# A hybrid attention block: the relative-position line is written to DRAM once, and the banded branch takes its query rows in falling order

## The chip, the core and the metric

The kernel runs on one core of a Trainium2 chip. The core has five engines that work side by side, each through its own queue in order: PE (TensorE, matrix products; PEld is its weight load), DVE (VectorE), ACT (ScalarE), POOL (GpSimd) and SP (SyncE, which here only issues DMAs; ACT's queue issues some as well). 16 DMA engines move the data. The metric is the device time of one run in microseconds (us); lower is better.

## What is computed

One block of a network on 512 tokens of width 1024, in float32. A normalised input is projected to four branches; each branch output is projected to 1024 columns, multiplied by a sigmoid gate of its own, and the four are added, projected once more and added to the input. A gated feed-forward layer of width 2816 follows. The branches are a softmax attention with a forget term ("fox", 4 heads), a short convolution, a chunked linear attention ("mlstm") and an attention in a sliding window of 128 tokens ("swa", 8 query heads, 2 key heads). The change is about the last one, whose scores have a bias that depends on the distance of query and key alone:

```
dist = arange(128)[:, None] + 128 - arange(256)[None, :]       # query row, key column of the band
swa_bias = rel_bias[t5_bucket(maximum(dist, 0))]                # per head, 128 x 256
s = q @ k_band.T * d**-0.5 + swa_bias                           # 4 blocks of 128 queries, 256 keys each
s = where(0 <= dist < 128 and key exists, s, -inf)
p = softmax(concat(s, sink))[..., :-1]
out = p @ v_band
```

A query in row i and a key in column j of the band have the distance i + 128 - j, so one line of 384 values per head, indexed by j - i + 127, holds every bias and the mask.

## The kernel before, in words

Every product of float32 data is made of three matmuls over split operands: a value is split into a rounded high part (`hi`, an ACT copy, L133) and the rest (`lo`, a DVE subtract, L134), and `mm3` (L127 to L130) multiplies hi by hi, hi by lo and lo by hi. Weights come as a stream of 512 KB tiles that SP loads into 3 buffers (`w_load`, L157); each tile has two halves that `w_split` splits on ACT and DVE, up to 6 halves ahead of use. A buffer takes the next load when both of its halves are split.

`proj` (L395) makes one block of 128 output columns for all 512 tokens: 8 steps of three matmuls of 512 columns. The order of the program is: the first projections (value and gate logits), fox keys and queries with their head norms (`head_normed`), the three conv projections `pcu`, `pcc`, `pcb` for two halves, the conv branch's gates (`gated("conv")`, tiles `gconv` for the gate and `oconv` for the branch output) with the fox attention running in the background, the swa keys and queries, the fox gates with the swa attention in the background, the mlstm projections, the swa gates, the mlstm gates, merge and feed-forward. The order on each engine's queue isn't that of the text: a planner simulates the program and sets the order of each queue; at run time each queue is worked off strictly in that order.

The bias line: `swa_bias_line` (L364) makes the 8 x 384 line with one matmul (`pl`), copies it to SBUF (`ln`), and one DMA on ACT's queue writes it 128 times into a DRAM tensor `d_line` of 128 x 8 x 384 (L371). The DMA's outer dimension is the 8 heads, each of which is one SBUF partition. `swa_bias_load` (L374), right ahead of the swa projections, loads four tiles `bw` of 128 x (2 heads x 256): partition i starts one element earlier in its own copy than partition i - 1 in its, so a row of 256 slides along the line (L377).

The swa queries: `q_stack` (L406) puts hi over lo for each head into a tile `sq..q` of 128 partitions by 512 tokens, with one ACT copy and one DVE subtract. In `swa_attention`, `scores` (L536) multiplies 128 queries (as the stationary operand) with the keys of the band, a DVE instruction adds the bias tile and takes the row maximum (L555), and exp, row sum and scaling follow; `transposes` (L574) turns the probabilities so that keys lie on the partitions; `values` (L583) multiplies them with the values, adds the two halves of the result on DVE (`sw`, L596) and splits the sum into the branch output `ysh`, `ysl` (L599), 128 tokens at a time.

Of the kernel before, what the change touches and what calls it, by code (L numbers as in the profile page):

```python
# [8 lines left out]
F32 = mybir.dt.float32  # L9
# [3 lines left out]
ALU = mybir.AluOpType  # L13
# [3 lines left out]
P = 128  # L17
# [10 lines left out]
LW = 384  # L28

FOX_H, ML_H, SWA_H, SWA_KV = 4, 4, 8, 2  # L30
# [14 lines left out]
def kernel(  # L45
# [11 lines left out]
    nc = tc.nc  # L57
# [4 lines left out]
    dram = ctx.enter_context(tc.tile_pool(name="dram", bufs=1, space=DRAM))  # L62
# [4 lines left out]
    def s_tile(name, dt=F32):  # L67
        return big.tile([P, NT], dt, tag="s", name=name, bufs=N_S)

    def wk(name, dt=F32):  # L70
        return big.tile([P, NT], dt, tag="wk", name=name, bufs=N_WK)
# [4 lines left out]
    def ps_at(name):  # L76
        return psum.tile([P, NT], F32, tag="at", name=name, bufs=8 - TUNE["mm"])
# [16 lines left out]
            else:  # L94
                nc.sync.dma_start(wr[-1], w_tok[ko // 2])

# [1 line left out]
    ident = const.tile([P, P], F32, name="ident")  # L98
    make_identity(nc, ident)
    ident_bf = const.tile([P, P], BF16, name="ident_bf")  # L100
# [18 lines left out]
    qgain = const.tile([P, 2], F32, name="qgain")  # L119
    nc.gpsimd.tensor_scalar(qgain[:, 0:1], col[:, C_FQ:C_FQ + 1], HD ** -0.5, None, op0=ALU.mult)  # L120
    nc.gpsimd.tensor_scalar(qgain[:, 1:2], col[:, C_SQ:C_SQ + 1], HD ** -0.5, None, op0=ALU.mult)

# [1 line left out]
    def nc_table(name):  # L124
        tc.keep_in_program_order(nc.scalar.preload_act_table_set(name))

# [5 lines left out]
    def split(hi, lo, src):  # L132
        nc.scalar.copy(hi, src)  # L133
        nc.vector.tensor_tensor(lo, src, hi.bitcast(F32), op=ALU.subtract)  # L134

    def scaled_split(hi, lo, src, scale):
        nc.scalar.activation(hi, src, AF.Copy, scale=scale)
        nc.vector.scalar_tensor_tensor(
            lo, src, scale, hi.bitcast(F32), op0=ALU.mult, op1=ALU.subtract)
# [5 lines left out]
        nc.vector.scalar_tensor_tensor(t, t, -0.5, v, op0=ALU.mult, op1=ALU.mult)  # L145
        nc.vector.scalar_tensor_tensor(out, t, 1.5, y0, op0=ALU.add, op1=ALU.mult)

# [1 line left out]
    n_w = w_str.shape[0]  # L149
    stream = {"raw": 0, "split": 0, "raws": [], "ready": []}  # L150

# [26 lines left out]
    def w_blk(w, j, n=P):  # L178
        return w[0][:, j * n:(j + 1) * n], w[1][:, j * n:(j + 1) * n]

    # work that rides along with the projections: `later` runs a piece after a number of
    # product steps, `background` advances one stage of an attention every `period` of them
    background, deferred = [], []
    pace = {"period": 4, "count": 0}

    def later(steps, fn):
        deferred.append([steps, fn])
# [24 lines left out]
        while len(background) > keep:  # L212
            bg()

    # ---- the array runs at its full clock once it has been busy for a while: keep it so
    # while the first loads are on their way ----
    warm = const.tile([P, NT], BF16, name="warm")
    nc.vector.memset(warm, 0.0)
    pw = ps_mm("warm_ps")
    for _ in range(TUNE["warm"]):  # L220
        nc.tensor.matmul(pw, warm[:, 0:P], warm, start=True, stop=True)

# [1 line left out]
    xg = []  # L224
    ssq = wk("ssq")
    ps_n = [ps_at(f"psn{t}") for t in range(NB)]
    for ko in range(KO):
# [7 lines left out]
        for t in range(NB):  # L235
            tb = slice(t * P, (t + 1) * P)
# [3 lines left out]
        else:  # L240
            sq = wk(f"xsq{ko}")
# [36 lines left out]
    nsnk = const.tile([P, SWA_H], F32, name="nsnk")  # L278
    nc.gpsimd.tensor_scalar(nsnk, snk, -1.0, None, op0=ALU.mult)

    # token-major results: fox v, swa v, gate logits
    vf = [s_tile(f"vf{t}", F32R) for t in range(NB)]
    vs2 = [s_tile(f"vs{i}", F32R) for i in range(2)]
    vs = [vs2[t // 2][:, (t % 2) * 256:(t % 2) * 256 + 256] for t in range(NB)]
# [3 lines left out]
    for t in range(NB):  # L288
        r1 = rcol[:, t:t + 1]
        for v, c0, n in ((vf[t], 0, FOX_H), (vs[t], 256, SWA_KV)):  # L290
            vv = v.rearrange("p (h u d) -> p h u d", h=n, u=2)
            src = ps_n[t][:, c0:c0 + n * HD].rearrange("p (h d) -> p h d", h=n)
# [2 lines left out]
        nc.vector.tensor_scalar(  # L295
            gdst, ps_n[t][:, 384:396].rearrange("p (a b) -> p a b", b=4), r1, None, op0=ALU.mult)

# [1 line left out]
    d_rows = dram.tile([12, NT], F32, name="d_rows")  # L299
    acol = const.tile([P, NB, 4], F32, name="acol")  # L300
    negc, negm, gexp = [], [], []
# [55 lines left out]
                    bass.AP(d_rows.tensor, d_rows.offset + (8 + 2 * p + j) * NT, [[0, HD], [1, NT]]))  # L357
            gexp.append(t)

# [1 line left out]
    d_line = dram.tile([P, SWA_H, LW], F32, name="d_line")  # L361
    biasw = []

    def swa_bias_line():  # L364
        pl = ps_at("pl")
        nc.tensor.matmul(pl[0:SWA_H, 0:LW], rb, oh, start=True, stop=True)
        ln = wk("ln")
        nc.vector.tensor_copy(ln[0:SWA_H, 0:LW], pl[0:SWA_H, 0:LW])
        src = ln[0:SWA_H, 0:LW]
        src = bass.AP(src.tensor, src.offset, [src.ap[0], [0, P], [1, LW]])  # L370
        nc.scalar.dma_start(d_line.rearrange("p h w -> h p w"), src)  # L371
        yield

    def swa_bias_load():  # L374
        for i in range(4):
            t = s_tile(f"bw{i}")
            nc.scalar.dma_start(  # L377
                t.rearrange("p (h k) -> p h k", h=2),
                bass.AP(d_line.tensor, d_line.offset + 127 + 2 * i * LW,
                        [[SWA_H * LW - 1, P], [LW, 2], [1, 256]]))  # L380
            biasw.append(t)

# [1 line left out]
    xn = []  # L384

    def normed_input(ko):
# [4 lines left out]
        scaled_split(h, l, t, col[:, C_AN + ko:C_AN + ko + 1])  # L391
        xn.append((h, l))

# [1 line left out]
    def proj(name, moving=None):  # L395
        ps = ps_mm(name)
        mv = moving or xn
        for ko in range(KO):
            if ko % 4 == 0:
                w = w_take()  # L400
            mm3(ps, w_blk(w, ko % 4), mv[ko], ko == 0, ko == KO - 1)
            tick()
        return ps

# [1 line left out]
    def q_stack(name, src, scale=1.0):  # L406
        out = []
        for j in range(2):
            own, oth = slice(j * HD, j * HD + HD), slice(HD - j * HD, P - j * HD)
            t = s_tile(f"{name}q{j}", F32R)  # L410
            if scale == 1.0:
                split(t[own], t[oth], src[own])
            else:
                scaled_split(t[own], t[oth], src[own], scale)
            out.append(t)
        return out
# [13 lines left out]
    def head_normed(name, ps, gain, eps, then):  # L430
        qg, sq = s_tile(f"{name}g"), s_tile(f"{name}s")
        nc.scalar.activation(sq, ps, AF.Square)
        nc.scalar.activation(qg, ps, AF.Copy, scale=gain)
        s2 = sum_split(name, sq)
        later(TUNE["norm_lag"], lambda: head_normed_rest(name, qg, sq, s2, eps, then))
# [20 lines left out]
        nc.gpsimd.tensor_tensor(qg, qg, sq, op=ALU.mult)  # L456
        then(qg)

# [1 line left out]
    y = {}  # L460

    def pt_split(name, src, n):
# [62 lines left out]
    def swa_attention():  # L525
        ysw = []
        for g in range(SWA_KV):
            t = [big.tile([P, 2, NT], F32R, tag="ysw", name=f"ys{n}{g}", bufs=4) for n in "hl"]
# [54 lines left out]
        def values(b, g):  # L583
            k0, nk = keys(b)
            po = ps_at(f"so{b}_{g}")
            for kk in range(nk):
                vv = vs[k0 // P + kk][:, g * P:(g + 1) * P]
                th = trans.pop((b, g, kk))
                nc.tensor.matmul(po, vv, th[0], start=kk == 0, stop=False)
                nc.tensor.matmul(po, vv, th[1], start=False, stop=kk == nk - 1)  # L590
            tmp, ys = wk(f"sv{b}_{g}"), wk(f"sw{b}_{g}")
            nc.scalar.copy(tmp[0:HD], po[HD:P])
            pov, tmv = (t.rearrange("p (i j t) -> p i j t", i=2, j=2) for t in (po, tmp))
            ysv = ys[:, 0:256].rearrange("p (i t) -> p i t", i=2)
            for j in range(2):
                nc.vector.tensor_tensor(ysv[j * HD:(j + 1) * HD], pov[0:HD, :, j, :], tmv[0:HD, :, j, :], op=ALU.add)  # L596
            yh, yl = ysw[g]
            tb = slice(b * P, (b + 1) * P)
            split(yh[:, :, tb], yl[:, :, tb], ysv)  # L599

        items = [(b, g) for b in range(NB) for g in range(SWA_KV)]
        yield from staged(items, (0, scores), (TUNE["swa_t"], transposes), (TUNE["swa_v"], values))
# [58 lines left out]
        items = [(2 * pair + j, b) for j in range(2) for b in range(NB)]  # L661
        yield from staged(items, (0, scores), (TUNE["ml_v"], values), (TUNE["ml_n"], normed))

# [1 line left out]
    y["fox"], y["conv"], y["swa"], y["mlstm"] = [], [], [], []  # L665
    fq, fk, sq_, sk, mq, mk, mo, vm = [], [], [], [], [], [], [], []
    gr, bl = gate_rows(), swa_bias_line()
# [5 lines left out]
    for p in range(2):  # L673
        ps = proj(f"pfk{p}", xg)
        head_normed(f"fk{p}", ps, col[:, C_FK:C_FK + 1], epsv, lambda k, p=p: fk.append(k_stack(f"fk{p}", k)))
        ps = proj(f"pfq{p}", xg)
        head_normed(f"fq{p}", ps, qgain[:, 0:1], epsv, lambda q, p=p: fq.append(q_stack(f"fq{p}", q)))

# [1 line left out]
    for p in range(2):  # L680
        ps = proj(f"pcu{p}")
        u = wk(f"cu{p}")
        nc.scalar.copy(u, ps)
        ps = proj(f"pcc{p}")
# [9 lines left out]
        ps = proj(f"pcb{p}")  # L694
        nc.vector.tensor_tensor(u, ps, u, op=ALU.mult)
        yh, yl = s_tile(f"ych{p}", F32R), s_tile(f"ycl{p}", F32R)
# [35 lines left out]
    gated("conv", False)  # L732
    flush()

# [1 line left out]
    swa_bias_load()  # L736
    nc_table("natural_log_exp_and_others")
    ps = proj("psk")
    head_normed("sk", ps, col[:, C_SK:C_SK + 1], None, lambda k: sk.extend(k_stack("sk", k)))
    for p in range(4):  # L740
        ps = proj(f"psq{p}")
        head_normed(f"sq{p}", ps, qgain[:, 1:2], None, lambda q, p=p: sq_.append(q_stack(f"sq{p}", q)))

    gated("fox", False, TUNE["swa_p"], swa_attention)

# [1 line left out]
    wv = [w_take() for _ in range(4)]  # L747
    for t in range(NB):
        ps = ps_mm(f"pmv{t}")
        tb = slice(t * P, (t + 1) * P)  # L750
        for ko in range(KO):
            w = wv[ko // 2]
# [7 lines left out]
        src = ps[:, 0:256].rearrange("p (g u d) -> p g u d", g=2, u=2)  # L760
# [4 lines left out]
    for p in range(2):  # L765
        ps = proj(f"pmk{p}")
        mk.append(k_stack(f"mk{p}", ps))
        ps = proj(f"pmq{p}")
        mq.append(q_stack(f"mq{p}", ps, HD ** -0.5))
        ps = proj(f"pmo{p}")  # L770
        t = s_tile(f"mo{p}")
# [8 lines left out]
    flush()  # L780
    gated("mlstm", True)

# [1 line left out]
    x2, x2g = [], []  # L784
    ssq2 = wk("ssq2")
    for d in range(KO):
        xr = wk(f"xr{d}")
        nc.scalar.dma_start(xr, xT[d * P:(d + 1) * P, :])
        ps = proj(f"mg{d}", merged)
        t = s_tile(f"x2_{d}")  # L790
# [7 lines left out]
        else:  # L798
            sq = wk(f"x2sq{d}")
            nc.scalar.activation(sq, t, AF.Square)  # L800
            nc.gpsimd.tensor_tensor(ssq2, ssq2, sq, op=ALU.add)

# [1 line left out]
    r2 = s_tile("r2")  # L804
    act = []
    for f in range(FB):
# [13 lines left out]
    w, j = None, 0  # L820
    for d in range(KO):
        ps = ps_mm(f"dn{d}")
        for f in range(FB):
            if j % 4 == 0:
                w = w_take()
# [3 lines left out]
        n = NT // 2 if d == KO - 1 else NT  # L829
# [11 lines left out]
def _layout(inputs):  # L841
    import numpy as np

    i = {k: np.asarray(v) for k, v in inputs.items()}
# [65 lines left out]
    cols[32:36, C_GB] = i["mlstm_f_bias"][0]  # L910
    cols[64:68, C_GB] = i["mlstm_i_bias"][0]

    # bucket of each distance: depends on shapes alone
    oh = np.zeros((33, LW), np.float32)
    n = np.arange(P)
    large = 16 + (np.log(np.maximum(n, 1).astype(np.float32) / np.float32(16))
                  / np.float32(np.log(8.0)) * np.float32(16)).astype(np.int32)
    bucket = np.where(n < 16, n, np.minimum(large, 31))
# [33 lines left out]
```

## Time and profile before

| what | value |
|---|---|
| time, median of 3 runs | 872.1 us (871.13 to 874.33) |
| span of the profiled execution, first to last instruction | 871.3 us |
| PE busy | 850.4 us (98%) |
| DVE busy | 493.5 us (57%) |
| ACT busy | 385.7 us (44%) |
| POOL busy | 145.1 us (17%) |
| mean granted TensorE clock | 0.990 |
| HBM read, written | 84.53 MB, 3.69 MB |

The profile gives the profiled execution by its span. A busy PE is one with a matmul in it, at whichever clock was granted (1.0 is 2.4 GHz, 0.5 is 1.2 GHz). Idle time of an engine costs something only where the work that sets the end waits for it; the table averages over stages with different limits.

### The profile page before, as it was taken

What the parts mean: (1) busy time and instruction counts of PE and PEld (TensorE: products, weight loads), DVE (VectorE), ACT (ScalarE), POOL (GpSimd) and SP (SyncE); (2) the same over time, 40 slices, a digit from 0 to 9 for tenths busy, and PEclk for the clock granted to TensorE, in tenths of its full rate; (3) what the DMA queues carried; (4) which work ended last, traced back from release to release, by engine and by line L of the source; (5) the groups of instructions that cost most, each with busy time, mean ns of one, the idle gap of its engine ahead of it and who ended that gap; (6) DMA issues with size and microseconds to landing.
All of it is one profiled execution on the core that took longest, in us unless ns stands there. A gap on an engine that the chain in (4) does not pass through costs nothing.

```text
span 871.3 us, 10668 instructions
## 1 busy us (share of the span) xinstructions
PE 850.4 (98%) x3879; PEld 701.1 (80%) x3879; DVE 493.5 (57%) x899; ACT 385.7 (44%) x733; POOL 145.1 (17%) x134
## 2 busy tenths in 40 slices
PE   7999799999999999999999999999999999999998
PEld 5867578888788888888888888888888888888886
DVE  6899576548888886577644545444444433432320
ACT  7565455457665765454544444333333322322210
POOL 5253000013311101222221212111111111000000
PEclk9999899999999999999999999999999999999999
DMA  6644422242222422222224432222222322233310
GB/s 229 212 145 86 109 97 73 73 145 73 73 73 72 147 73 96 73 74 97 96 97 128 151 108 97 98 97 97 97 97 97 97 96 97 97 121 108 121 37 24
DMA packets 29537, 88.91 MB, mean 102 GB/s; under 512 B 3456, under 2 KB 6049, under 8 KB 29485
## 3 DMA queue, kind: packets, MB, share of 16 engines
q1 hardware_dynamic: 24716, 80.87, 27.5%
q10 hardware_dynamic: 4768, 7.37, 3.8%
q8 instruction: 30, 0.49, 0.2%
q14 instruction: 23, 0.18, 0.1%
HBM read 84.53 MB, written 3.69 MB: 101 GB/s over the span
## 4 chain that ended last, share of the span: by engine, by line
PE 83%; DVE 7%; DMA 3%; ACT 2%; issue 2%; SPq 0%; POOL 0%; DVEq 0%; ACTq 0%; POOLq 0%
PE dn L130 5%; PE fu L130 5%; PE fg L130 5%; PE dn L129 5%; PE fu L128 5%; PE fg L128 5%; PE fu L129 5%; PE fg L129 5%; PE dn L128 5%; DMA wr<-in_w_str_dram 2%; PE gswa L129 2%; PE gswa L128 2%; PE gswa L130 2%; PE gmlstm L128 2%; PE gmlstm L130 2%
## 5 line engine op out<-in xcount | busy, mean ns | idle before, releaser
L134 DVE TENSOR_TENSOR wl<-wr,wh 128x512 fp32r<-128x512 f32 x278 | 202.9, 733 | 163.9 <-ACT wh L133 162.6
L133 ACT CAST wh<-wr 128x512 fp32r<-128x512 f32 x278 | 170.3, 619 | 273.5 <-PE dn L129 69.1
L129 PE MATMUL fu<-x2l,wh 128*128 128x512 f32 x176 | 68.5, 389 | 0.0
L128 PE MATMUL fu<-x2h,wh 128*128 128x512 f32 x176 | 68.5, 389 | 0.0
L130 PE MATMUL fg<-x2h,wl 128*128 128x512 f32 x176 | 68.5, 389 | 0.0
L130 PE MATMUL fu<-x2h,wl 128*128 128x512 f32 x176 | 68.5, 389 | 0.0
L128 PE MATMUL fg<-x2h,wh 128*128 128x512 f32 x176 | 68.5, 389 | 0.0
L129 PE MATMUL fg<-x2l,wh 128*128 128x512 f32 x176 | 68.5, 389 | 0.0
L128 PE MATMUL dn<-ah,wh 128*128 128x512 f32 x176 | 68.5, 389 | 0.0
L129 PE MATMUL dn<-al,wh 128*128 128x512 f32 x176 | 68.5, 389 | 0.0
L130 PE MATMUL dn<-ah,wl 128*128 128x512 f32 x176 | 68.5, 389 | 0.0
L815 POOL TENSOR_TENSOR ut<-ut,gt 128x512 f32<-128x512 f32 x22 | 34.3, 1560 | 204.6 <-DVE ut L814 175.7
L130 PEld LDWEIGHTS fg<-x2h,wl 128*128 128x128 f32 x176 | 33.1, 188 | 6.9
L129 PEld LDWEIGHTS fu<-x2l,wh 128*128 128x128 f32 x176 | 33.1, 188 | 6.9
L128 PEld LDWEIGHTS dn<-ah,wh 128*128 128x128 f32 x176 | 33.0, 188 | 6.9
L129 PEld LDWEIGHTS dn<-al,wh 128*128 128x128 f32 x176 | 33.0, 188 | 6.9
L129 PEld LDWEIGHTS fg<-x2l,wh 128*128 128x128 f32 x176 | 33.0, 188 | 6.9
L128 PEld LDWEIGHTS fu<-x2h,wh 128*128 128x128 f32 x176 | 33.1, 188 | 6.8
L130 PEld LDWEIGHTS fu<-x2h,wl 128*128 128x128 f32 x176 | 33.0, 187 | 6.9
L130 PEld LDWEIGHTS dn<-ah,wl 128*128 128x128 f32 x176 | 33.0, 188 | 6.7
L128 PEld LDWEIGHTS fg<-x2h,wh 128*128 128x128 f32 x176 | 33.0, 188 | 6.7
L814 DVE TENSOR_TENSOR ut<-fu,r 128x512 f32<-128x512 f32 x22 | 15.2, 691 | 29.9 <-PE fu L130 29.9
(598 smaller groups left out, 1936.0 us busy)
## 6 DMA issues: line engine op xcount, KB each, us to landing
wr<-in_w_str_dram SPq DMA_DIRECT2D x139, 512.0 KB, 3.2
xc<-in_xT_dram SPq DMA_DIRECT2D x8, 256.0 KB, 5.8
xs<-in_xT_dram SPq DMA_DIRECT2D x8, 256.0 KB, 3.9
xr<-in_xT_dram ACTq DMA_DIRECT2D x8, 256.0 KB, 2.6
out_dram<-o SPq DMA_DIRECT2D x7, 256.0 KB, 2.1
d_line<-ln ACTq DMA_DIRECT2D x1, 1536.0 KB
wnr<-in_w_tok_dram SPq DMA_DIRECT2D x3, 396.0 KB, 6.1
negc<-d_rows ACTq DMA_DIRECT2D x4, 256.0 KB, 5.1
```

The costliest lines, as they stand in the source:

```text
L128: nc.tensor.matmul(out, a[0], b[0], start=start, stop=False)
L129: nc.tensor.matmul(out, a[0], b[1], start=False, stop=False)
L130: nc.tensor.matmul(out, a[1], b[0], start=False, stop=stop)
L133: nc.scalar.copy(hi, src)
L134: nc.vector.tensor_tensor(lo, src, hi.bitcast(F32), op=ALU.subtract)
L814: nc.vector.tensor_tensor(ut, pu, r2, op=ALU.mult)
L815: nc.gpsimd.tensor_tensor(ut, ut, gt, op=ALU.mult)
```

## The change

The line is written once: `d_line` has 8 x 384 values, and the DMA on ACT's queue copies the 8 rows of `ln` into it. All 128 partitions of a bias tile then read from this one line, partition i from element i on, so the step from one partition to the next is +1 (it was a whole copy less one element). Partition i so holds the bias of query 127 - i of its block. To match, the query tiles of the swa branch are filled in falling order within each block of 128 tokens (`falling=True`), with a view that walks the destination backwards, and the branch output is read backwards before it is split, so that it stands in rising order again. Scores, softmax, transposes and value products work on the reversed rows unchanged. The rest of the diff takes out comment lines.

```diff
-    d_line = dram.tile([P, SWA_H, LW], F32, name="d_line")
+    d_line = dram.tile([SWA_H, LW], F32, name="d_line")
...
-        src = ln[0:SWA_H, 0:LW]
-        src = bass.AP(src.tensor, src.offset, [src.ap[0], [0, P], [1, LW]])
-        nc.scalar.dma_start(d_line.rearrange("p h w -> h p w"), src)
+        nc.scalar.dma_start(d_line, ln[0:SWA_H, 0:LW])
...
-                bass.AP(d_line.tensor, d_line.offset + 127 + 2 * i * LW,
-                        [[SWA_H * LW - 1, P], [LW, 2], [1, 256]]))
+                bass.AP(d_line.tensor, d_line.offset + 2 * i * LW,
+                        [[1, P], [LW, 2], [1, 256]]))
...
+    def rev(t):
+
+        n = t.shape[-1]
+        return bass.AP(t.tensor, t.offset + P - 1, [t.ap[0], [P, n // P], [-1, P]])
+
+    def q_stack(name, src, scale=1.0, falling=False):
...
-            if scale == 1.0:
+            if falling:
+                s3 = src[own].rearrange("p (b t) -> p b t", t=P)
+                hi, lo = rev(t[own]), rev(t[oth])
+                nc.scalar.copy(hi, s3)
+                nc.vector.tensor_tensor(lo, s3, rev(t.bitcast(F32)[own]), op=ALU.subtract)
+            elif scale == 1.0:
...
-            tb = slice(b * P, (b + 1) * P)
-            split(yh[:, :, tb], yl[:, :, tb], ysv)
+            ysr = bass.AP(ysv.tensor, ysv.offset + P - 1, [ysv.ap[0], ysv.ap[1], [-1, P]])
+            split(yh[:, :, b * P:(b + 1) * P], yl[:, :, b * P:(b + 1) * P], ysr)
...
-        ... sq_.append(q_stack(f"sq{p}", q)))
+        ... sq_.append(q_stack(f"sq{p}", q, falling=True)))
```

## Rows read from the trace of the kernel before

**Rows 1.** Stretches: length, busy us (instructions) per engine, granted clock, DMA share, GB/s

```profile
94.70:104.00 9.30, 6.09 (x15) 4.81 (x16) 6.88 (x11) 5.05 (x9) 1.19 (x1) 0.63 0.48 107
104.00:117.30 13.30, 9.46 (x41) 6.93 (x40) 12.83 (x37) 8.59 (x21) 0.09 (x1) 0.87 0.34 117
117.30:215.00 97.70, 97.70 (x466) 80.26 (x465) 61.08 (x123) 54.00 (x108) 9.67 (x7) 1.00 0.28 92
500.00:700.00 200.00, 200.00 (x884) 165.58 (x883) 87.92 (x134) 73.38 (x119) 29.66 (x20) 1.00 0.29 98
```

**Rows 2.** The chain that ended last, 60 to 116 us: start, us, what

```profile
76.36 19.47 DMA wr<-in_w_str_dram
```

**Rows 3.** The weight tiles' view: the 139 loads

```profile
DMA to landing us min/median/max: 3.1/3.2/19.5
```

**Rows 4.** DMA issues of the whole run: line, operation, KB each

```profile
d_line<-ln ACTq DMA_DIRECT2D x1, 1536.0 KB
```

**Rows 5.** Stretches as in rows 1, two short ones

```profile
72.00:76.00 4.00, 4.00 (x19) 3.29 (x18) 3.88 (x8) 3.94 (x8) 0.19 (x1) 1.00 0.43 52
...
102.00:103.00 1.00, 1.00 (x4) 0.81 (x3) 0.97 (x3) 0.00 (x0) 0.19 (x1) 0.50 0.45 52
```

**Rows 6.** Timeline of ACT: start, us, instruction, idle before and what ended it

```profile
83.90 0.72 ACT L691 ACTIVATE cu<-cz,col 128x512 f32<-128x512 f32 x1 [0.40 <-DVE cz L686]
95.91 0.62 ACT L133 CAST wh<-wr 128x512 fp32r<-128x512 f32 x1 [11.28 <-DMA wr<-in_w_str_dram]
96.43 0.62 ACT L142 ACTIVATE fq1s<-fq1v 128x512 f32<-128x512 f32 x1
```

**Rows 7.** Timeline of DVE

```profile
86.25 0.68 DVE L454 SCALAR_TENSOR_TENSOR fq1v<-fq1m,epsv 128x512 f32<-128x512 f32 x1
86.85 1.39 DVE L693 SCALAR_TENSOR_TENSOR cu<-cz,col,cu 128x510 f32<-128x510 f32 x1
96.56 0.69 DVE L134 TENSOR_TENSOR wl<-wr,wh 128x512 fp32r<-128x512 f32 x1 [8.32 <-ACT wh L133]
...
98.26 0.42 DVE L424 CAST fk1a<-fk1a 64x512 fp32r<-64x512 f32 x1 [0.41 <-ACT fk1a L423]
...
114.17 0.47 DVE L492 TENSOR_SCALAR fp<-fp,fst 128x512 f32<-128x512 f32 x1
```

**Rows 8.** Timeline of PE

```profile
97.91 0.80 PE L128 MATMUL gconv<-xnh,wh 128*128 128x512 f32 x1 [3.21 <-DVE cu L695]
...
108.46 0.50 PE L129 MATMUL oconv<-ycl,wh 128*128 128x512 f32 x1 [1.87 <-DVE ycl L134]
...
112.51 0.33 PE L499 MATMUL ft<-ident,fp 128*128 128x128 f32 x1 [1.51 <-DVE fp L492]
...
114.70 0.69 PE L499 MATMUL ft<-ident,fp 128*128 128x128 f32 x2 [0.46 <-DVE fp L492]
115.04 0.78 PE L130 MATMUL gconv<-xnh,wl 128*128 128x512 f32 x1
```

**Rows 9.** Timeline of POOL

```profile
86.41 1.29 POOL L456 TENSOR_TENSOR fk1g<-fk1g,fk1s 128x512 f32<-128x512 f32 x1 [7.03 <-DVE fk1s L146]
```

**Rows 10.** DMA issues with median us to landing; issue and first use of the band

```profile
negc<-d_rows ACTq DMA_DIRECT2D x4, 256.0 KB, 5.1
bw<-d_line ACTq DMA_DIRECT2D x4, 256.0 KB, 3.6
...
L377 ACTq DMA_DIRECT2D bw<-d_line x4: 399/488/749, 182.6 to 184.3; - x4
...
L555 DVE CUSTOM_DVE_ANT_0 sp<-ss,bw x32: 277/417/425, 233.3 to 291.8; 128x256 f32<-128x256 f32 x24, 128x128 f32<-128x128 f32 x8
```

**Rows 11.** Groups by shape, 200 to 315 us: busy us, mean ns, idle before

```profile
L134 DVE TENSOR_TENSOR sq2q<-sq2g,sq2q 64x512 fp32r<-64x512 f32 x2 | 1.4, 687 | 0.1
L134 DVE TENSOR_TENSOR ysl<-sw,ysh 128x256 fp32r<-128x256 f32 x6 | 2.5, 417 | 0.0
...
L133 ACT CAST sq2q<-sq2g 64x512 fp32r<-64x512 f32 x2 | 1.2, 618 | 2.7 <-POOL sq2g L456 2.7
```

More of the change, by code (lines that the diff above doesn't have):

```diff
@@ L403, in proj @@
         return ps
-    def q_stack(name, src, scale=1.0):
+    def rev(t):
+        n = t.shape[-1]
+        return bass.AP(t.tensor, t.offset + P - 1, [t.ap[0], [P, n // P], [-1, P]])
+    def q_stack(name, src, scale=1.0, falling=False):
         out = []
@@ L741 @@
         ps = proj(f"psq{p}")
-        head_normed(f"sq{p}", ps, qgain[:, 1:2], None, lambda q, p=p: sq_.append(q_stack(f"sq{p}", q)))
+        head_normed(f"sq{p}", ps, qgain[:, 1:2], None, lambda q, p=p: sq_.append(q_stack(f"sq{p}", q, falling=True)))
     gated("fox", False, TUNE["swa_p"], swa_attention)
```

## The prediction

> **What bounds the kernel now.** I read the profile from coarse to fine: busy time per stretch, the chain of work that ended last, the DMA view, and then the queues of ACT, DVE and PE one after another in the one place where they stop.
>
> The stretches first [rows 1]. From 117.3 us on PE is busy for 97.70 of 97.70 us and later for 200.00 of 200.00 us at full clock: PE sets the end there, and whatever brings the state of 117.3 us forward brings the end forward. Just before it PE is badly fed: between 94.7 and 104 us it works 6.09 of 9.30 us at a mean granted clock of 0.63, between 104 and 117.3 us 9.46 of 13.30 us at 0.87. No other stretch that this change touches has such a hole.
>
> The chain of waits names who made the hole: 19.47 us of one weight load that was issued at 76.36 us [rows 2]. The median load of that kind lands 3.2 us after its issue, and 19.5 us is the longest of all 139 [rows 3]. What ran beside it is the write of the relative-position line: one issue on ACT's queue, 1536 KB [rows 4]. Before any weight load joins it, that write alone holds 0.43 of the 16 DMA engines' time and moves 52 GB/s, and at 102 to 103 us it still holds 0.45 at the same 52 GB/s [rows 5]. So it occupies about half of the engines from about 71.5 to 103.5 us (1.57 MB at some 50 GB/s is 31 us), and a weight load that is spread over all of them ends only when its part on that half has come through.
>
> ACT shows the price [rows 6]: its cast of the loaded weights stands right behind an activation that ends at 83.90 + 0.72 = 84.62 us, and starts at 95.91 us after 11.28 us of waiting for the load; everything in ACT's order behind it (the norm of the fox queries) waits too. DVE, in order as well, ends its last free instruction at 86.85 + 1.39 = 88.24 us, then sits 8.32 us behind that cast [rows 7]. PE still has projections to run until about 94.7 us; then its gate product waits 3.21 us for a PSUM tile that a DVE instruction behind the stalled one frees [rows 8]. From there on PE waits for DVE three more times that matter: 1.87 us at the conv output product, 1.51 us at a fox transpose and 0.46 us at another.
>
> **The change part by part.**
>
> *The line written once.* The write shrinks from 1536 KB to 12 KB, from 1024 rows of 1536 B to 8. At the old pace of 50 GB/s that is 0.25 us of half the engines, ahead of the load at 76.36 us by more than 4 us. The matmul, the copy to SBUF and the single issue on ACT's queue stay. The load at 76.36 us then lands at 76.36 + 3.2 = 79.6 us; the next ones have the engines for themselves too. What follows, step by step, with every queue in its present order:
>
> - ACT's cast runs at 84.62 instead of 95.91 us. The next ACT instruction, on fq1, needs a DVE result that ends at 86.25 + 0.68 = 86.93 us, so ACT loses no time to the DMA at all and is then paced by DVE.
> - DVE goes on at 88.24 instead of 96.56 us: 8.32 us gained. Its short wait of 0.41 us for ACT's fk1a goes as well: that cast came 1.83 us after fq1s began (96.43 to 98.26), so it is done by 86.93 + 1.83 = 88.8 us; its input from POOL ends at 86.41 + 1.29 = 87.70 us [rows 9]; DVE needs it only at 88.24 + (98.26 - 96.56 - 0.41) = 89.53 us. Instead of 98.26, that is 8.73 us gained, and from there DVE is busy almost without a break up to 117 us (12.83 of 13.30 us in the last stretch of rows 1), so it keeps this lead and no more.
> - PE ends its projections at 94.70 us as before and finds the PSUM tile free: the wait of 3.21 us goes and no slow clock follows it. The 24 gate matmuls up to the conv output product take 24 x 0.226 = 5.4 us (0.226 is 200.00 us over 884 matmuls, rows 1), so PE is at 100.1 us. The product's second matmul, at 108.46 us before, needs DVE at 108.46 - 8.73 = 99.7 us: PE comes at 100.1 + 0.23 = 100.4 us, and the wait of 1.87 us goes too.
> - What is late next is DVE again, at the fox transposes. PE needs ten matmuls, 2.3 us, and stands there at 102.6 us; DVE is ready at 112.51 - 8.73 = 103.8 us, a wait of 1.2 us. The last one of the stretch, at 114.64 us (114.17 + 0.47), becomes 105.9 us. The five gate matmuls behind it ran at the lower level (2.3 us from 115.04 to 117.3 us); I leave them so, since the same gaps stand ahead of them.
> - So the state of 117.3 us comes at 108.6 us: 8.7 us. If the clock stays up there, five matmuls at 0.226 take 1.1 us less: 9.8 us.
>
> By the Trainium skill (DMA: Bandwidth & Descriptors, "Rules for kernel authors") a transfer of 1 MiB or more is what reaches the bandwidth and one under 64 KB is mostly overhead, which speaks for the big write and against the small one; at the 341 GB/s that its table has for 1 MB, the old write would take an estimated 4.6 us, be over at 76 us and cost the load nothing, and the sum would be 0. The trace disagrees: 52 GB/s [rows 5] and 19.47 us [rows 2].
>
> *The band read with rising steps.* Four loads of 256 KB as before, but 128 partitions now read overlapping pieces of one 12 KB area instead of 128 separate copies. No row of before shows these pieces; the nearest are the loads that broadcast one 2 KB row to all partitions, 5.1 us to landing, and the present band loads, 3.6 us [rows 10]. I take up to 1.5 us more. A gain is worth nothing, as the first reader starts at 233.3 us, while the loads are issued from 182.6 us; that span of 47 us also covers the loss. The upper end is the pace of the old write: 1 MB at 52 GB/s is 20 us, still before 233 us, but weight loads issued beside it would then be late as at 76 us.
>
> *Queries and outputs in falling order.* The number of instructions stays: for each of 8 query tiles one ACT copy and one DVE subtract, for each of 8 output blocks one ACT copy and one DVE subtract, each with one operand (the subtract for queries with two) walked backwards in runs of 128. They take 0.687 us on DVE and 0.618 on ACT for a query tile, and 0.417 on DVE for an output block [rows 11]; its ACT copy I take as long. Nothing in the trace is walked backwards. As many elements pass, so there is nothing to gain; if a falling step halved the pace and nothing hid it, the cost would be 8 x (0.687 + 0.618 + 0.417 + 0.417) = 17.1 us. I take 0, the nearest rows being these same instructions with the same counts. PE, the transposes and the bias add see the same shapes.
>
> *Sum.* -8.7 + 0 + 0: the profiled span of 871.3 us becomes 862.6 us. The median of the three runs, 872.1, is 0.8 us above that span, so the run should read 863.4 us.
>
> **The rivals.**
>
> *A, everything of the hole comes back.* If DVE's order eases as well, PE gets back its 3.21 us, the 3.84 us idle after 104 us (13.30 - 9.46), the slow clock of the first stretch (15 matmuls in 6.09 us, 3.4 us at 0.226: 2.7 us) and of the second (1.1 us): 10.8 us, 861.3 us. Against it: DVE is 96% busy in the second stretch.
>
> *B, part is given back.* The order of every queue comes from a planner that simulates the program; with a smaller write it may order DVE and ACT differently, and DVE has no slack before 117 us. Then only the wait before the gate product and the slow clock behind it are sure, 3.2 + 2.7 = 5.9 us, and a misplaced instruction or two takes 1 to 2 us of that: 866 to 868 us. For it: DVE has no free time in which to make up a bad order. Against it: the present order already puts ACT's cast at 84.6 us, as if no load were late.
>
> *C, the write isn't what holds the load.* Then the wait stays: 872 us. Against it: 3.2 us for the median load and half of the engines busy before the load begins.
>
> *D, slower.* Falling operands run at half pace or less. Place: the stretch from 210 to 315 us, where DVE forms the query tiles right before the scores. Price up to 17.1 - 8.7 = 8.4 us: 880 us; it turns the gain into a loss from the point where 8.7 of the 17.1 us are exposed. For it: no row shows such a step. Against it: ACT stands idle for 2.7 us ahead of one pair of these copies, waiting for POOL [rows 11], so a part would be hidden.
>
> **How the numbers follow.** The forecast has 0.62 (862 to 865.5 us), A 0.13, B 0.17, C 0.04, D 0.04. The range takes the forecast, the upper gain of 9.8 to 10.8 us and the better part of B: 860 to 867.5 us. Half a per cent, 4.4 us, is what I take a measurement to tell from no change: below 867.7 us are the forecast, A and most of B (0.62 + 0.13 + 0.12), within it the rest of B and C (0.09), above it D (0.04).
>
> **What would show it.** Right: the 1536 KB issue is 12 KB; between 72 and 76 us the DMA share is near 0; the longest weight load lands within some 6 us; ACT's wait of 11.28 us and DVE's of 8.32 us are gone, the gate product starts near 94.7 us at full clock, a wait of about 1 us for DVE stays at the fox transposes, and the stretch between 94.7 us and full PE is about 14 instead of 22.6 us. The query and output splits keep 0.69, 0.62 and 0.42 us. Wrong: a weight load still over 10 us, the same idle time on DVE at another place before 117 us, splits that take longer, or weight loads beside the band loads that ACT waits for.

## The result, and the profile after

The changed kernel takes 862.99 us (median of 4 runs, 862.29 to 863.43) against 872.25 us for the kernel before (4 runs): ratio 0.9885, 95% interval 0.9872 to 0.9897, so 1.2% faster. Forecast were 863.4 us and a range of 860.0 to 867.5. The profiled execution has a span of 861.1 us and a run time of its own of 862.88 us, 1.8 us more. The profile before has no run time of its own beside its span of 871.3 us; if as much lies around it, that execution took some 873.1 us, an estimate from these figures and 0.9 us more than the median. That would account for the spans differing by 10.2 us and the medians by 9.3.

The stretches after, with the columns of [rows 1], the fifth with those of [rows 5]:

```profile
94.70:104.00 9.30, 8.81 (x40) 6.91 (x38) 9.18 (x26) 6.85 (x16) 0.34 (x1) 1.00 0.30 98
104.00:117.00 13.00, 12.40 (x64) 10.02 (x64) 10.41 (x29) 8.02 (x19) 0.00 (x0) 1.00 0.34 116
117.30:215.00 97.70, 97.56 (x464) 80.21 (x463) 63.17 (x117) 54.79 (x104) 14.42 (x10) 1.00 0.27 88
500.00:700.00 200.00, 200.00 (x884) 165.55 (x883) 85.80 (x132) 71.30 (x115) 29.04 (x19) 1.00 0.28 96
...
72.00:76.00 4.00, 4.00 (x19) 3.31 (x18) 3.91 (x8) 3.26 (x6) 0.49 (x1) 1.00 0.00 0
```

The hole is closed: between 94.7 and 104 us PE works 8.81 of 9.30 us at full clock where it had 6.09 at 0.63, and from 107 us on it is full, which was so from 117.3 us on. From 72 to 76 us no DMA moves at all (0.43 before). Later stretches keep their pace: 884 matmuls in 200.00 us in both kernels. The compute instructions come in the same order as before on every engine, one by one, and so do the weight loads on SP's queue; so nothing here is due to the planner.

The DMA view answers to [rows 4, 10]: the traffic of ACT's queue (4768 packets and 7.37 MB before), the band loads and the write; the weight tiles' view answers to [rows 3].

```profile
q10 hardware_dynamic: 3752, 5.81, 2.3%
...
bw<-d_line ACTq DMA_DIRECT2D x4, 256.0 KB, 3.7
...
d_line<-ln ACTq DMA_DIRECT2D x1, 12.0 KB
```

```profile
DMA to landing us min/median/max: 3.0/3.3/7.6
```

The three loads issued at 76.06, 80.25 and 84.20 us land in 3.2 to 3.3 us. The longest, 7.6 us, is none of them.

The queues at the place of the hole, ACT, DVE and PE, answer to [rows 6 to 8]:

```profile
84.23 0.61 ACT L133 CAST wh<-wr 128x512 fp32r<-128x512 f32 x1
86.73 0.63 ACT L142 ACTIVATE fq1s<-fq1v 128x512 f32<-128x512 f32 x1 [1.89 <-DVE fq1v L462]
```

```profile
86.55 1.41 DVE L701 SCALAR_TENSOR_TENSOR cu<-cz,col,cu 128x510 f32<-128x510 f32 x1
87.89 0.68 DVE L134 TENSOR_TENSOR wl<-wr,wh 128x512 fp32r<-128x512 f32 x1
...
89.20 0.42 DVE L432 CAST fk1a<-fk1a 64x512 fp32r<-64x512 f32 x1
...
105.12 0.48 DVE L500 TENSOR_SCALAR fp<-fp,fst 128x512 f32<-128x512 f32 x1
```

```profile
94.87 0.39 PE L128 MATMUL gconv<-xnh,wh 128*128 128x512 f32 x1
...
100.54 0.39 PE L129 MATMUL oconv<-ycl,wh 128*128 128x512 f32 x1
...
103.46 0.33 PE L507 MATMUL ft<-ident,fp 128*128 128x128 f32 x1 [0.49 <-DVE fp L500]
...
105.65 0.44 PE L507 MATMUL ft<-ident,fp 128*128 128x128 f32 x2 [0.60 <-DVE fp L500]
105.84 0.48 PE L130 MATMUL gconv<-xnh,wl 128*128 128x512 f32 x1
...
107.09 0.39 PE L129 MATMUL gconv<-xnl,wh 128*128 128x512 f32 x1
```

The last of these is the first gate matmul from which PE is full; in the kernel before it is this one:

```profile
117.28 0.39 PE L129 MATMUL gconv<-xnl,wh 128*128 128x512 f32 x1
```

ACT casts the tile as soon as it is free and then waits for DVE; DVE runs on without a gap; PE has no wait left in front of `gconv` and `oconv`, and two short ones for DVE at the fox transposes.

The groups with falling operands, answering to [rows 11] (the query splits now have lines of their own, L417 and L418):

```profile
L418 DVE TENSOR_TENSOR sq2q<-sq2g,sq2q 64x512 fp32r<-64x512 f32 x2 | 1.4, 686 | 0.1
L134 DVE TENSOR_TENSOR ysl<-sw,ysh 128x256 fp32r<-128x256 f32 x6 | 2.5, 418 | 0.0
...
L417 ACT CAST sq2q<-sq2g 64x512 fp32r<-64x512 f32 x2 | 1.2, 618 | 2.7 <-POOL sq2g L464 2.7
```

686, 418 and 618 ns against 687, 417 and 618: an operand walked backwards costs the same here. The band loads above land in 3.7 us against 3.6.

### The profile page after: what moved, and what is told of

It is laid out like the page before. It is cut to its first block, busy times and chain, and to the rows that moved or that the text cites. A ratio compares the mean times of both kernels' runs of the same rounds, so it can differ in the third digit from the quotient of the medians.

```text
span 861.1 us, 10668 instructions
## 1 busy us (share of the span) xinstructions
PE 846.6 (98%) x3879; PEld 699.6 (81%) x3879; DVE 493.4 (57%) x899; ACT 386.1 (45%) x733; POOL 144.9 (17%) x134
## 4 chain that ended last, share of the span: by engine, by line
PE 84%; DVE 8%; ACT 3%; issue 2%; DMA 2%; SPq 0%; POOL 0%; DVEq 0%; ACTq 0%; POOLq 0%
PE dn L130 5%; PE fu L128 5%; PE dn L129 5%; PE fg L128 5%; PE fu L130 5%; PE fg L130 5%; PE fu L129 5%; PE fg L129 5%; PE dn L128 5%; PE gswa L129 2%; PE gswa L128 2%; PE gswa L130 2%; PE gmlstm L128 2%; PE gmlstm L130 2%; PE mg L130 2%
```

## The experiments

The theory: all of the gain is the 128-fold write no longer standing beside the weight load of 76 us, and the loss is set by when that load lands against the instant at which ACT wants it. The rivals: the falling order or the band's new step carry part of the gain; or the loss simply goes with the bytes written. The first four runs shared a chip and the runs of the kernel before (873.35 us there, 13 runs), the next three another group (872.29 us), the last two a third (872.88 us).

**The write put back.** In the changed kernel the line is written 128 times again, and partition i reads its own copy:

```diff
-    d_line = dram.tile([SWA_H, LW], F32, name="d_line")
+    d_line = dram.tile([P, SWA_H, LW], F32, name="d_line")
...
-        nc.scalar.dma_start(d_line, ln[0:SWA_H, 0:LW])
+        src = ln[0:SWA_H, 0:LW]
+        src = bass.AP(src.tensor, src.offset, [src.ap[0], [0, P], [1, LW]])
+        nc.scalar.dma_start(d_line.rearrange("p h w -> h p w"), src)
...
-                        [[1, P], [LW, 2], [1, 256]]))
+                        [[SWA_H * LW + 1, P], [LW, 2], [1, 256]]))
```

> The changed kernel with the 128-fold write put back (each partition reads its own copy, one element further on than its neighbour); queries and outputs stay in falling order. Theory (all of the gain is the write no longer standing beside the weight load that is issued at 76 us): the gain is gone, 872 us, with a weight load of some 19 us, ACT waiting some 11 us and DVE some 8 us. Rival (the falling order or the band's rising step brings part of it): clearly under 872, 864 to 869 us.

Measured: 871.65 us, ratio to before 0.9984 (0.9974 to 0.9993). The longest weight load takes 20.7 us, and ACT waits as before; the second line is the matmul from which PE is full:

```profile
96.48 0.62 ACT L133 CAST wh<-wr 128x512 fp32r<-128x512 f32 x1 [12.55 <-DMA wr<-in_w_str_dram]
```

```profile
116.72 0.40 PE L129 MATMUL gconv<-xnl,wh 128*128 128x512 f32 x1
```

The loss is back, but for 1.7 us (0.6 to 2.3 by the interval) against 873.35 us. That rest isn't the falling order or the rising step, as far as the profiles show: both act only after 182 us [rows 10], and from the matmul above to the end of the span it takes 754.0 us in all three kernels (871.3 - 117.28 before, 870.7 - 116.72 here, 861.1 - 107.09 in the changed kernel). The single write carries the gain; where the 1.7 us come from stays open.

**The falling order taken out.** The changed kernel with queries and outputs in rising order:

```diff
-... q_stack(f"sq{p}", q, falling=True)
+... q_stack(f"sq{p}", q)
...
-            split(yh[:, :, b * P:(b + 1) * P], yl[:, :, b * P:(b + 1) * P], ysr)
+            split(yh[:, :, b * P:(b + 1) * P], yl[:, :, b * P:(b + 1) * P], ysv)
```

> The changed kernel with the queries and outputs left in rising order, so that only the single write of the line and the loads from it are new (the bias tile then lies reversed against the query rows: the attention of the banded branch is computed with the wrong bias row, with the same work). Theory: as the changed kernel, 863 us, within 1 us. Rival (a falling operand costs time that is exposed, up to 17 us by the prediction's bound): faster than 863 by what it costs.

Measured: 863.9 us, ratio 0.9896 (0.9876 to 0.9916), not faster than the changed kernel; the interval is some 1.7 us either way. With the rows above, the falling order costs nothing that can be measured.

**Fewer copies.** The changed kernel with 32 and with 64 copies, of which the first is read (shown for 64):

```diff
-    d_line = dram.tile([SWA_H, LW], F32, name="d_line")
+    d_line = dram.tile([64, SWA_H, LW], F32, name="d_line")
...
-        nc.scalar.dma_start(d_line, ln[0:SWA_H, 0:LW])
+        src = ln[0:SWA_H, 0:LW]
+        src = bass.AP(src.tensor, src.offset, [src.ap[0], [0, 64], [1, LW]])
+        nc.scalar.dma_start(d_line.rearrange("p h w -> h p w"), src)
```

> The changed kernel with the line written 32 times; only the first copy is read. At the old pace of 0.24 us a copy the write runs from about 72 to 80 us. Theory (what counts is whether the load issued at 76 us lands before ACT reaches its cast at 84.2 us): the load takes 4 to 7 us instead of 3.3, ACT doesn't wait, 863 us. Rival (time goes with the bytes written): 9.3 us x 31/127 = 2.3 us lost, 865.3 us.

> The changed kernel with the line written 64 times; only the first copy is read. The write runs from about 72 to 88 us. Theory: the load issued at 76 us lands at 88 to 90 us, ACT's cast comes 4 to 5 us after 84.2 us, DVE idles about 2 us in front of it, 865 to 866 us. Rival (time goes with the bytes written): half of 9.3 us lost, 867.6 us.

Measured: 863.41 us with 32 copies, ratio 0.9896 (0.9878 to 0.9915), and 865.89 with 64, ratio 0.992 (0.9901 to 0.9939). The load of 76 us lands in 5.5 us with 32 copies and nobody waits for it. With 64 it takes 12.7 us, and ACT and DVE wait:

```profile
88.82 0.62 ACT L133 CAST wh<-wr 128x512 fp32r<-128x512 f32 x1 [4.51 <-DMA wr<-in_w_str_dram]
...
89.47 0.69 DVE L134 TENSOR_TENSOR wl<-wr,wh 128x512 fp32r<-128x512 f32 x1 [1.56 <-ACT wh L133]
```

The first quarter of the bytes is free and the second costs 2.5 us: what counts is the instant at which ACT wants the tile, not the bytes. The rival's 865.3 and 867.6 us are near enough that times alone wouldn't refuse it (0.9896 and 0.992 of 873.35 have intervals of some 1.7 us either way); the waits do.

**All 16 engines.** The kernel before, with the 8 rows standing twice on 16 partitions and 64 copies taken of each:

```diff
-        nc.tensor.matmul(pl[0:SWA_H, 0:LW], rb, oh, start=True, stop=True)
+        n16 = 2 * SWA_H
+        nc.tensor.matmul(pl[0:n16, 0:LW], rb, oh, start=True, stop=True)
...
-        src = bass.AP(src.tensor, src.offset, [src.ap[0], [0, P], [1, LW]])
-        nc.scalar.dma_start(d_line.rearrange("p h w -> h p w"), src)
+        src = bass.AP(src.tensor, src.offset, [src.ap[0], [0, P // 2], [1, LW]])
+        nc.scalar.dma_start(
+            bass.AP(d_line.tensor, d_line.offset, [[LW, n16], [n16 * LW, P // 2], [1, LW]]), src)
```

> The kernel before, its 128 copies written from 16 partitions (the 8 rows stand there twice) in place of 8, so that the DMA can be split over all 16 engines. Theory (the old write was slow because 8 source rows keep it on half of the engines at 52 GB/s): about 100 GB/s and a DMA share near 0.9, over at 88 us in place of 103; the load of 76 us lands near 89 us as with 64 copies, 865 to 868 us. Rival (something else, such as the writing into DRAM, sets the pace of 52 GB/s): the write still lasts 31 us, 870 to 873 us.

Measured: 866.28 us, ratio 0.9921 (0.9904 to 0.9939). Its stretches, in the columns of [rows 5]:

```profile
72.00:76.00 4.00, 3.63 (x17) 2.67 (x16) 3.88 (x8) 3.98 (x8) 0.01 (x1) 1.00 0.79 91
...
84.00:88.00 4.00, 3.71 (x18) 2.61 (x17) 4.00 (x7) 0.73 (x1) 1.28 (x1) 1.00 0.87 97
88.00:92.00 4.00, 4.00 (x19) 3.25 (x19) 1.10 (x3) 1.31 (x3) 0.00 (x0) 1.00 1.01 385
```

Same bytes, share 0.79 in place of 0.43 and 91 GB/s in place of 52 before any weight load is issued, and over soon after 88 us: the number of source rows set the pace, by way of the engines that take part. By the packets' times in the two traces, at most 8 packets of the old write are under way at once, and up to 16 of this one. The Trainium skill (DMA: Bandwidth & Descriptors, "Rules for kernel authors") says that an outermost dimension of fewer than 16 confines a DMA to at most that many engines; these two shares agree with it.

The trace shows something else here. Weight loads are issued at 76.54, 80.73 and 84.67 us, yet the DMA view of 77 to 88 us has packets of the write's queue alone, at 97 GB/s (packets, MB, share of 16 engines):

```profile
q10 hardware_dynamic: 696, 1.07, 87.1%
```

So these loads didn't share the engines with the write; they moved when it was over (385 GB/s from 88 to 92 us), and ACT still waited 5.9 us for one. What was gained came from the write being over sooner.

**A deeper lead.** The kernel before with a fourth buffer for raw weights:

```diff
-    "n_s": 58, "n_wk": 11, "w_raw": 3, ...
+    "n_s": 56, "n_wk": 11, "w_raw": 4, ...
```

> The kernel before with 4 raw weight buffers in place of 3 (and 56 in place of 58 general tiles, to make room); the 128-fold write stays. Each weight load is issued one buffer release earlier, so the tile that ACT casts at 84 us is loaded before the write begins, and it is the next one that comes late. Theory: a load of some 19 us is still there, but ACT meets it at the cast of 90 us and waits about 5 in place of 11 us: 864 to 868 us. Rival (the lead of the loads is no part of it): 870 to 873 us.

Measured: 864.73 us, ratio 0.9907 (0.9885 to 0.9929). A load still takes 19.5 us, but the tile of the cast at 83.51 us is there; the next one is late:

```profile
94.91 0.62 ACT L133 CAST wh<-wr 128x512 fp32r<-128x512 f32 x1 [4.80 <-DMA wr<-in_w_str_dram]
```

So most of the gain can be had with the write left as it was, by one more load in flight. (SP's order of loads, and late in the program that of DVE and ACT, change a little; up to 95 us the picture is that of the theory.)

**The write later.** The kernel before, with the line made and written around 113 us, where DVE has time to spare:

```diff
-    later(40, lambda: next(bl, None))
...
+    later(24, lambda: next(bl, None))
     gated("conv", False)
     flush()
```

> The kernel before, its 128-fold write issued later, after the third gate product of the conv branch (around 110 to 115 us), in a stretch where DVE has time to spare (14 of 23 us busy between 117 and 140 us in place of 98%). Theory (31 us of a half-busy DMA cost only what the engine behind them can't make up): weight loads of 15 to 20 us there as well, but DVE and ACT catch up while PE lives on its lead: 863 to 868 us. Rival (the write costs its 9 us wherever it stands): 870 to 873 us.

Measured: 880.67 us, ratio 1.0088 (1.0071 to 1.0106): slower than before, and neither the theory's time nor the rival's. Besides a weight load that ACT waits 7.36 us for, the trace shows a wait that I hadn't thought of; the chain, then ACT:

```profile
113.54 32.70 DMA d_line<-ln
```

```profile
146.32 0.48 ACT L133 CAST fx_1h<-ft 128x384 fp32r<-128x384 f32 x1 [8.30 <-DMA d_line<-ln]
```

The write holds its source, a tile of the pool with 11 buffers, for as long as it runs, and a split of the fox attention wants that buffer. The planner's order differs too. Two more kernels take these apart. They have the queue orders of this one, the second but for the line's own copy and write, which stand three instructions later on DVE and ACT (the write is issued at 116.13 in place of 113.54 us). The first writes the line once at the late place (the changed kernel with the edit above):

> The changed kernel (single write, falling order) with the line made and written at the later place, around 113 us; every queue has the same order as in the kernel with the late 128-fold write (880.7 us). It tells the price of the 128-fold write at that place from the price of the other order that the planner made for it. Theory: by the trace of the late 128-fold write PE idles 5.9 us more between 130 and 150 us and runs some 3.4 us longer for the slow clock behind it, about 9 us; so 870 to 872 us here, and the other 8 us over the changed kernel are the order (among them 5 us of waits for ACT at the fox gates). Rival (the late write itself is dearer, the order is harmless): 863 to 866 us.

The second keeps the 128-fold write and moves its source to the pool with 58 buffers:

```diff
-        ln = wk("ln")
+        ln = s_tile("ln")
```

> The kernel with the late 128-fold write, its source line in a tile of the pool with 58 buffers in place of the pool with 11. In the late version ACT waited 7.4 us for a weight load and then 8.3 us more for the buffer of the line, which the write holds for 32.7 us and a split of the fox attention takes over. Same order on all queues. Theory: the second wait goes, the weight loads stay slow (18 us), 3 to 7 us are regained of 880.7: 874 to 878 us. Rival (the held buffer only takes the place of a wait that is there anyway): 879 to 881 us.

Measured: 870.72 us, ratio 0.9975 (0.9966 to 0.9985), and 874.82 us, ratio 1.0022 (1.0013 to 1.0032). The 17.7 us between the changed kernel and the late 128-fold write are then 7.7 us for the other order (870.72 - 862.99), 5.9 us for the held buffer (880.67 - 874.82, with whatever the later place of the write is worth) and 4.1 us for the slow weight loads (874.82 - 870.72). The first two differences go over two groups of runs. The other order shows at the fox gates, here with the line written once late; before, the first of these was 0.8 us:

```profile
PE gfox L128 <- ACT tfox L724: 3.8, 1, 3.8
...
PE gfox L128 <- ACT sq2g L441: 2.2, 1, 2.2
```

So slow loads did cost less there, where DVE has slack, 4.1 in place of about 9 us; but the theory's "863 to 868 us" left out the two other prices of moving a step.

## Why the prediction was right, step by step

- *PE sets the end after 117 us, so the shift of that state is the gain.* Right. The gate matmul that stood at 117.28 us stands at 107.09 us, 10.19 us earlier, and the span is 10.2 us shorter.
- *The write occupies half of the engines and holds the load of 76 us.* Right, shown from both sides: put back, the loss returns but for 1.7 us; over 16 engines, the share nearly doubles.
- *ACT at 84.62, DVE at 88.24, PE's gate product at 94.7, the conv output's second matmul at 100.4 us.* Measured 84.23, 87.89, 94.87 and 100.54.
- *DVE gains 8.73 us.* The scaling that stood at 114.17 us [rows 7] stands at 105.12: 9.05 us earlier, of which 0.30 us were there ahead of the place (86.55 for 86.85 us). They belong to the two executions, not to the change: the copy of the line, ahead of the write, already starts at 70.40 for 70.69 us. The step itself: 8.75 us.
- *DVE is late next, 1.2 us at the fox transposes.* Right in kind, smaller in the profiled execution: 0.49 us, since DVE came 0.3 us earlier than reckoned and PE 0.35 us later (102.97 for 102.6 us); the second wait is 0.60 us (0.46 before). Two other kernels in which nobody waits for a weight load at this place, the one with rising order and the one with 32 copies, have 1.11 and 1.10 us, near the forecast. PE came some 0.65 us later against DVE than in those two (its gate product 8.32 us behind the DVE instruction of 86.55 us, there 7.68 and 7.67 us), after a stretch from 60 to 72 us at a mean granted clock of 0.72, in place of 1.00; that this made it late is likely, not shown.
- *The slow clock of the five matmuls stays.* Not in the profiled execution, and that is the term that was mis-sized for it: after the last transpose PE ran at the full level, 1.25 us from 105.84 to 107.09 us in place of 2.24, and the transposes just before them took 0.15 us less. The prediction has both cases, 8.7 and 9.8 us, and took the first, "since the same gaps stand ahead of them". The runs don't bear that reason out. Idle times of 1.11 and 0.60 us stand ahead in the kernel with rising order, where the lower level is back, and of 1.10 and 0.60 us in the one with 32 copies, where it isn't. The first wait and the stretch from 106 to 108 us, in the columns of [rows 1], for these two:

```profile
103.16 0.33 PE L507 MATMUL ft<-ident,fp 128*128 128x128 f32 x1 [1.11 <-DVE fp L500]
...
106.00:108.00 2.00, 2.00 (x6) 1.52 (x6) 1.67 (x8) 1.81 (x6) 0.00 (x0) 0.50 0.48 195
```

```profile
103.91 0.33 PE L509 MATMUL ft<-ident,fp 128*128 128x128 f32 x1 [1.10 <-DVE fp L502]
...
106.00:108.00 2.00, 1.91 (x10) 1.60 (x11) 1.66 (x9) 1.06 (x4) 0.00 (x0) 1.00 0.77 262
```

Their spans, 862.4 and 861.5 us, lie 8.9 and 9.8 us under the 871.3 us of before: both cases of the prediction occur. With 64 copies, idle 1.33, 1.49 and 0.60 us, the lower level is back as well (0.63 us a matmul record in place of 0.39). What decides stays open, so this term of the forecast was a guess, whichever way it came out.

- *Band and falling order cost 0.* Right, by the rows and by the second experiment. The price allowed for the band, up to 1.5 us to landing, was 0.1 us (3.7 for 3.6 us); the 17.1 us bounded for the falling order don't show at all.
- *Sum.* 8.75 for DVE, 0.30 ahead of it, 0.99 + 0.15 for the clock behind it: 10.19 us in the profiles. In medians it is 9.3 us; the profiled execution before was probably one of the slower ones. The forecast of 8.7 us lies 0.6 us under the medians.
- The rivals: A (everything comes back) asked for 10.8 us and is nearest in the profile, yet DVE still sets the fox transposes. B fell, as the planner's order didn't change. C and D fell. The prediction sets 52 GB/s against the Trainium skill's rule of 1 MiB or more and its 341 GB/s; that rule and that figure are for 128 partitions, and the write comes from 8, so the trace doesn't speak against them.
- The signs: the longest weight load is 7.6 us, over the 6 us named, but none of those at the hole; from 94.70 us to full PE it is 12.4 us, for the 14 named. The wait at the fox transposes is half of the 1 us named; the other signs of being right came.

## What to carry to other kernels

Read the landing times of the loads beside a DMA's share, and not its megabytes: a transfer whose outer dimension is 8 rows kept half of the engines for 31 us, and the weight loads issued beside it came up to 16 us late. What it costs is then settled by who is first to need the late tile: an in-order queue passes the delay on to everything behind it, so 32 copies were free, 64 cost 2.5 us and 128 cost 9. A fourth weight buffer, one more load in flight, hid most of it; moving the transfer elsewhere made it worse, since the DMA also held its source buffer for as long as it ran and the planner wrote a new order around the moved step.

## What was not expected of the hardware

Operands walked backwards in float32 ran at the same pace on ACT (618 ns) and DVE (686 and 418 ns). 128 partitions that read overlapping 1 KB pieces of one 12 KB area landed as fast as from 128 separate copies (3.7 and 3.6 us). And 1.57 MB from 8 rows took 32.70 us in the late version, where the chain shows the write's whole length: 48 GB/s, while from 16 rows it moved at 91 to 97 GB/s. Nor did the weight loads get a share of the engines beside that write: from 77 to 88 us not one of their packets moved.
